# Hybrid scan and pooling block on one core: output weights kept in halves, transpositions queued behind a matmul, and two scan operations moved from GpSimd to VectorE

## The chip, the cores and the metric

The kernel runs on one core of one Trainium2 chip. The metric is the time on the device of one execution, in microseconds (us); the median of several executions is compared.

## What is computed

One layer of a hybrid block over 2048 tokens of 1024 channels (with 256 context tokens that only give the scan its initial state). In a short form, batch and context left out:

```python
h = modulate(rmsnorm(x, pre_norm_mix), shift, scale)
proj = h @ w_in                                   # z | x,B,C | dt | pooled channels
xs, bm, cm = split(silu(dwconv(proj[xBC], conv_w)))      # 5 taps, centred
y_f, _ = ssd_chunked(xs, dt_f, a_f, bm, cm, h0_f)         # chunks of 128, forward
y_b, _ = ssd_chunked(reversed ...)                         # the same, backward
y = rmsnorm((y_f + y_b + d_skip * xs) * silu(z), ssm_norm)
p = pool_mixer(proj[pool], w_pool, pool_scale)    # box means of 2, 4, 8, 16 on a 32 x 64 grid
yx = concat([y, p]) @ w_out                       # 1024 x 1024
x = x + gate1 * rmsnorm(yx, post_norm_mix)
h2 = modulate(rmsnorm(x, pre_norm_ffn), ...)
x = x + gate2 * rmsnorm((silu(g) * v) @ w_down)   # v, g = split(dwconv(h2 @ w_up)), 3 taps
```

In a chunked scan the state of a chunk is the state before it times a decay for each head, plus what the chunk adds; the output of a chunk is an inner part plus `C @ state`, scaled by a decay.

## The kernel before

**Products.** All large products are made of fp32 numbers split in a high and a low half in the type fp32r: `hi` is a copy in that type, `lo` the difference. `mm3` (line 152) makes a product of three matmuls: high by high, high by low, low by high. `split` (120) makes the halves: the copy on ScalarE where `he` is S, else on VectorE, the subtraction on the engine `le`. `wunit` (127) loads one unit of 128 x 1024 weights through SP into a buffer "w" (seven of them, `NW`), copies on ScalarE (line 122) and subtracts on GpSimd (line 125). With `kept` and `first` the halves are also stored in DRAM through SP (141); with `kept` and not `first` nothing is split, and the halves are loaded (143), each into its buffer "w". The input weights are used in this way (`win`, 148: block 0 stores, blocks 1 to 3 load). The output weights aren't kept: each of their 32 uses loads, copies and subtracts.

**Forward part.** The tokens are worked on in four blocks of 512, from 0 to 3. For each block the rows are normalised and transposed, multiplied with the input weights, convolved on VectorE (`conv`), and the four chunks of the scan follow (`chunks`, 499), spread between the matmuls of the next block. In `chunks`, `states` (464) makes what a chunk adds to the state and calls `step` (458), which multiplies the old state with its decay on GpSimd (460) and adds on VectorE (462). `y_off` (485) multiplies C with the state on TensorE, scales the result on VectorE (492) and adds it to y on GpSimd (493). y, the chunks' backward states, silu(z) and the pooled rows go to DRAM (`y_d`, `sb_d`, `sz_d`, `p_d`). Pooling (`pool_mix`, 589) is done beside the last block.

**Backward pass with the output projection.** Blocks 3 to 0. `back_load` (844) loads a block's y, states, C and silu(z) through SP. `back` (861) goes through its four chunks from the last to the first: `y_off` with the backward state, `step`, the multiplication with silu(z) on VectorE (873), squares on ScalarE (874); then a scaling of the rows (877). The rows are transposed (969), split into `hxh` and `hxl` (972), and multiplied with the output weights, two halves `hh` of 512 channels by four units of two `k` each. For block 3 the four pooled units come first, in a loop of their own (950 to 958), since pooling ends earlier than the scan. Behind each block `Post.finish` (824) makes x1 and stores it in `x1_d`; `norm_x1` (897) normalises x1 for the feed-forward and transposes it (910), spread between the next block's matmuls; for blocks 3 to 1 it writes `h_d`, which `quarter_sums` (887) and `load_operand` (931) read. `load_operand` brings a 128 x 512 piece into a buffer of "raw", "t512" (three) or "cacc" (three) by turns (`stage`, 923) and splits it into an operand `xc`. Operand T4 lies in the buffer "XB", which holds block 0's x1 rows before.

**Feed-forward.** `up_pair(1, i)` (1058) multiplies 22 pairs of weight units with the operands of blocks 2 and 3, in seven products each. The first takes the weights as they are, the second and others take sums of them, which VectorE makes into buffers "t512" and "cacc" (1067 to 1071). Block 0's rows are only normalised here: `norm_late(i)` (1038), four times, each in two steps placed behind a pair (1174 to 1182): the first loads x1 rows into a buffer "xr", squares them on ScalarE (1043) and scales them on VectorE (1045); the second transposes eight times on TensorE (1052), scales on ScalarE (1053) and stores.

**Order.** The order in which the source issues instructions isn't the order on an engine. A planner with a simulated time line orders each engine's instructions, by priority and by when it believes them ready; `hot()` (117) raises the priority by 500. On the chip each engine then runs its instructions in that order, and so does SP with its transfers.

Of the kernel before, what the change touches and what calls it, by code (L numbers as in the profile page):

```python
# [9 lines left out]
F32 = mybir.dt.float32  # L10
# [10 lines left out]
P = 128  # L21
# [4 lines left out]
TB = 512  # L26
NB = SEQ // TB
# [25 lines left out]
def hybrid_block(ctx: ExitStack, tc: tile.TileContext, x, cx, ccol, crow, par, rowpar, cst, edge,  # L53
                 w_ada_a, w_ada_b, w_in, w_dt, w_pool, w_out, w_up, w_down, out):
    nc = tc.nc
    V, S, G, PE = nc.vector, nc.scalar, nc.gpsimd, nc.tensor
# [14 lines left out]
    dp = ctx.enter_context(tc.tile_pool(name="dp", bufs=1, space=DRAM))  # L71
# [55 lines left out]
    def wunit(src, le=G, kept=None, first=True):  # L127
# [15 lines left out]
                        nc.sync.dma_start(out=t.bitcast(F32), in_=d_)  # L143
        return hi, lo

    wk_d = [[dp.tile([P, 1024], F32, name=f"wk_d{m}_{s}") for s in range(2)] for m in range(16)]

    def win(m, b):
# [3 lines left out]
    def mm3(o, lt, rt, start, stop, **kw):  # L152
        PE.matmul(o, lt[0], rt[0], start=start, stop=False, **kw)  # L153
        PE.matmul(o, lt[0], rt[1], start=False, stop=False, **kw)  # L154
        PE.matmul(o, lt[1], rt[0], start=False, stop=stop, **kw)  # L155

    def rstd(ss, n, d, p=P):

# [109 lines left out]
    ADD, MUL, SUB = ALU.add, ALU.mult, ALU.subtract  # L268
# [163 lines left out]
    def b64(ap):  # L432
        return ap.unsqueeze(2).to_broadcast([P, H, 64])
# [4 lines left out]
    def hv(ap):  # L438
        return ap.rearrange("p (h e) -> p h e", h=H)
# [17 lines left out]

    def step(new, old, dec, add):

        G.tensor_tensor(out=hv(new), in0=hv(old), in1=b64(dec), op=MUL)  # L460
        for dst, a in add:
            V.tensor_tensor(out=new[:, dst], in0=a, in1=new[:, dst], op=ADD)

# [21 lines left out]
    def y_off(ct, i, d, q, st, y):  # L485

        ps = pb()
        for g in range(2):
            PE.matmul(ps[:, g * 256:(g + 1) * 256], ct[:, g, :], st[:, g * 256:(g + 1) * 256],
                      start=True, stop=True)  # L490
        t = t512()[:, 0:DS]
        V.tensor_tensor(out=hv(t), in0=hv(ps), in1=b64(q["ecs"][:, d, i, :]), op=MUL)
        G.tensor_tensor(out=y, in0=y, in1=t, op=ADD)

    carry = {}

# [241 lines left out]
    for b in range(NB):  # L738
# [49 lines left out]
        for kk in range(KD // 2):  # L788
            u = win(12 + zord[2 * kk] // 2, b)
# [6 lines left out]
        for i in range(4):  # L796
            o = cacc()
# [121 lines left out]
    xc = {}  # L919
# [30 lines left out]
    for hh in range(2):  # L950
        po = quarters()
        for n_, k in enumerate((7, 6, 5, 4)):
            if n_ % 2 == 0:
                u = wunit(w_out[4 * hh + k // 2])
            for i in range(4):
                mm3(po[i], hx(k, 2 + i * P, 2 + (i + 1) * P), ut(u, k % 2, 512), n_ == 0, n_ == 3)
        for i in range(4):
            S.copy(out=ys[i][:, hh * 512:(hh + 1) * 512], in_=po[i])
    split_psum(NU2)

    for b in range(NB - 1, -1, -1):
# [26 lines left out]
        for hh in range(2):  # L988
            hs = slice(hh * 512, (hh + 1) * 512)
            kord = DN[4:] if b == NB - 1 else DN  # L990
            po = quarters()
            for n_ in range(0, len(kord), 2):
                u = wunit(w_out[4 * hh + kord[n_] // 2])
                for ip in (0, 2):
                    for k in kord[n_:n_ + 2]:
                        for i in (ip, ip + 1):
                            mm3(po[i], hx(k, 2 + i * P, 2 + (i + 1) * P), ut(u, k % 2, 512),
                                k == kord[0], k == kord[-1])
                if n_ or hh:
                    next(ngen, None)  # L1000
                    next(ngen, None)
                if b == 0 and n_ % 4 == 2:
                    load_operand(1, NAMES[2 * hh + n_ // 4])
            if b == NB - 1:
                for i in range(4):
                    with hot():
                        V.tensor_tensor(out=ys[i][:, hs], in0=po[i], in1=ys[i][:, hs], op=ADD)
                po = [ys[i][:, hs] for i in range(4)]
            pst.half(hh, po)
# [48 lines left out]
    def up_pair(p, i):  # L1058
# [16 lines left out]
        def product(o, a, n, start, stop):  # L1075

            with hot():
                w = wtile(F32R, "wo")
                if isinstance(a, int) and not p:
                    nc.sync.dma_start(out=w.bitcast(F32), in_=wu_d[i][a - 1])  # L1080
                else:
                    split(w[:, 0:512], w[:, 512:1024], sums[a - 1] if isinstance(a, int) else a, S, V)
            if isinstance(a, int) and p:
                G.dma_start(out=wu_d[i][a - 1], in_=w.bitcast(F32))
            for kk in range(4):
                ks = slice(kk * P, (kk + 1) * P)
                mm3(o, (w[:, 0:512][:, ks], w[:, 512:1024][:, ks]), (xc[n][:, kk, 0:TB], xc[n][:, 4 + kk, 0:TB]),
                    start and kk == 0, stop and kk == 3, skip_group_check=True)

        o = 1 - p  # L1090
# [18 lines left out]
        n = 2 * TB + o  # L1109
        acc = []  # L1110
        for j, u, a in zip((i, NFF + i), un, (wide("av", 2), stile([P, D + 4], "cr"))):
# [9 lines left out]
            for t in (1, 2):  # L1121
                V.scalar_tensor_tensor(out=a[:, 0:n], in0=u[:, t:t + n], scalar=pt[:, cw + t:cw + t + 1],  # L1122
                                       in1=a[:, 0:n], op0=MUL, op1=ADD)
# [47 lines left out]

    for n in NAMES[4:]:
        load_operand(1, n)
    side = []
    for i in range(4):
        side += [norm_late(i)] * 2
    for n_, i in enumerate(j + h * NK for j in range(NK) for h in range(2)):
        up_pair(1, i)
        if 1 <= n_ <= 8:
            next(side[n_ - 1])  # L1180
        if n_ in (12, 14, 16, 18):
            left_sums(n_ // 2 - 6)
    for n in NAMES:
# [193 lines left out]
```

## Time and profile before

| | before |
|---|---|
| median of 3 runs | 2281.81 us (2278.71 to 2284.29) |
| profiled execution, its own time | 2280.55 us |
| its span in the trace | 2278.8 us |
| mean granted clock of TensorE | 0.969 |
| busy: TensorE, VectorE, ScalarE, GpSimd | 2120.4, 1652.3, 899.0, 574.0 us |
| moved by transfers | 552.93 MB, 243 GB/s over the span |

A time in the trace counts from the span's start. The profile names TensorE's matmuls PE, its weight loads PEld, VectorE DVE, ScalarE ACT, GpSimd POOL and SyncE SP; L462 is line 462 of the kernel. "wl<-wst,wh" is an instruction that writes tile wl and reads wst and wh. An arrow "<-" behind an idle time names what ended it, as far as the semaphores tell. A clock of 1.00 is the higher of TensorE's two levels (2.4 GHz), 0.50 the lower (1.2 GHz), and a value between is a mean of the two over a stretch.

### The profile page before, as it was taken

Reading aid. Unit: us, or ns where it says so; the run is one execution under the profiler, and the core shown is the slowest. Engines: PE = TensorE matmul, PEld = TensorE weight load, DVE = VectorE, ACT = ScalarE, POOL = GpSimd, SP = SyncE. Lnnn points to the kernel's source line nnn. Section 1 sums busy time; section 2 is a strip of 40 time slices with the busy share of each in tenths; the row PEclk is TensorE's granted clock in tenths of the full one; section 3 lists DMA queues with packets and bytes.
Section 4 is the critical chain, followed back from the end, with each engine's and each line's share of the span. In section 5 each row is a group of like instructions: output and inputs, shape, how many; then the busy total and the mean of one; then the engine's idle time right before and its main releaser. Section 6 shows DMA issues by size and latency. Waiting matters only on the chain.

```text
span 2278.8 us, 27562 instructions
## 1 busy us (share of the span) xinstructions
PE 2120.4 (93%) x9473; PEld 1675.8 (74%) x9473; DVE 1652.3 (73%) x2500; ACT 899.0 (39%) x1405; POOL 574.0 (25%) x811
## 2 busy tenths in 40 slices
PE   8898999799679888599999998999999999999998
PEld 4695777687457666388888887888888888888876
DVE  5778779977678767688888977777777763333676
ACT  4334342333325545445444445333333333333433
POOL 1443624535355443111223210111111110000000
PEclk9899999899899999799999999999999999999999
DMA  7857969768765658755578657789898884444484
GB/s 298 276 205 255 302 216 365 254 224 280 254 231 171 223 196 316 245 218 197 213 250 292 233 201 261 264 296 330 300 331 294 301 289 142 146 141 139 146 272 141
DMA packets 250044, 552.93 MB, mean 243 GB/s; under 512 B 52976, under 2 KB 101808, under 8 KB 249392
## 3 DMA queue, kind: packets, MB, share of 16 engines
q1 hardware_dynamic: 212272, 425.86, 55.5%
q0 software_dynamic: 32320, 121.12, 13.6%
q10 hardware_dynamic: 5312, 4.20, 0.5%
q8 instruction: 74, 1.21, 0.2%
q14 instruction: 66, 0.54, 0.1%
HBM read 369.56 MB, written 181.54 MB: 242 GB/s over the span
## 4 chain that ended last, share of the span: by engine, by line
PE 55%; DMA 4%; DVE 3%; ACT 1%; issue 1%; POOL 0%; SPq 0%; ACTq 0%; DVEq 0%; POOLq 0%
PE pu L154 16%; PE pu L155 16%; PE pu L153 16%; PE pb L153 2%; PE pb L154 2%; PE pb L155 2%; DMA wst<-in_w_out_dram 1%; DMA h_d<-t 1%; DMA res<-x_d 0%; DMA XB<-h_d 0%; DVE accd L1258 0%; DVE accd L1240 0%; DMA stg<-ds_d 0%; DMA t<-ds_d 0%; DVE hxl L125 0%
## 5 line engine op out<-in xcount | busy, mean ns | idle before, releaser
L153 PE MATMUL pu<-xcT,wo 128*128 128x512 f32 x704 | 280.1, 398 | 0.4 <-ACT xcT L122 0.4
L154 PE MATMUL pu<-xcT,wo 128*128 128x512 f32 x704 | 279.4, 397 | 1.0 <-DVE xcT L125 1.0
L155 PE MATMUL pu<-xcT,wo 128*128 128x512 f32 x704 | 277.8, 396 | 0.0
L125 DVE TENSOR_TENSOR as<-ar,as 128x1024 fp32r<-128x1024 f32 x66 | 80.8, 1225 | 192.9 <-ACT as L122 192.8
L153 PE MATMUL pu<-xcB,wo 128*128 128x512 f32 x528 | 205.8, 397 | 4.7 <-ACT e L1096 4.7
L154 PE MATMUL pu<-xcB,wo 128*128 128x512 f32 x528 | 209.3, 396 | 0.0
L155 PE MATMUL pu<-xcB,wo 128*128 128x512 f32 x528 | 208.6, 397 | 0.0
L122 ACT CAST wo<-rawu 128x512 fp32r<-128x512 f32 x132 | 80.8, 621 | 238.3 <-PE pu L155 238.1
L153 PE MATMUL pu<-wh,hxh 128*128 128x512 f32 x384 | 152.4, 414 | 17.7 <-ACT wh L122 9.6
L154 PE MATMUL pu<-hxl,wh 128*128 128x512 f32 (+2 forms) x448 | 166.2, 372 | 2.9 <-DVE hxl L125 2.8
L155 PE MATMUL pu<-hxh,wl 128*128 128x512 f32 (+2 forms) x448 | 166.1, 373 | 2.0 <-POOL wl L125 2.0
L153 PE MATMUL pu<-hxh,wh 128*128 128x512 f32 (+2 forms) x448 | 165.2, 373 | 2.5 <-ACT wh L122 1.4
L125 POOL TENSOR_TENSOR wl<-wst,wh 128x1024 fp32r<-128x1024 f32 x48 | 118.9, 2477 | 186.5 <-ACT wh L122 173.5
L154 PE MATMUL pu<-wl,hxh 128*128 128x512 f32 x384 | 158.7, 413 | 6.8 <-POOL wl L125 6.8
L155 PE MATMUL pu<-wh,hxl 128*128 128x512 f32 x384 | 155.2, 412 | 2.7 <-DVE hxl L125 2.7
L153 PEld LDWEIGHTS pu<-xcT,wo 128*128 128x128 f32 x704 | 132.7, 188 | 33.4 <-ACT xcT L122 0.8
L154 PEld LDWEIGHTS pu<-xcT,wo 128*128 128x128 f32 x704 | 132.6, 188 | 33.4 <-DVE xcT L125 1.3
L155 PEld LDWEIGHTS pu<-xcT,wo 128*128 128x128 f32 x704 | 132.3, 188 | 32.4
L122 ACT CAST as<-ar 128x1024 fp32r<-128x1024 f32 x66 | 69.2, 1048 | 217.2 <-PE pb L155 211.4
L1122 DVE SCALAR_TENSOR_TENSOR av<-un,pt,av 128x1024 f32<-128x1024 f32 (+1 forms) x88 | 113.0, 1284 | 31.0 <-ACT av L1119 16.7
L330 DVE SCALAR_TENSOR_TENSOR cacc<-raw,pt,cacc 128x512 f32<-128x512 f32 (+1 forms) x152 | 132.4, 875 | 3.7
L154 PE MATMUL pu<-tc,as 128*128 128x512 f32 x330 | 130.6, 396 | 0.0
(374 smaller groups left out, 4947.7 us busy)
## 6 DMA issues: line engine op xcount, KB each, us to landing
wu_d<-wo POOLq DMA_DIRECT2D x88, 512.0 KB, 3.2
wo<-wu_d SPq DMA_DIRECT2D x88, 512.0 KB, 5.0
rawu<-in_w_up_dram SPq DMA_DIRECT2D x66, 512.0 KB, 4.9
wh<-wk_d SPq DMA_DIRECT2D x48, 512.0 KB, 7.2
wl<-wk_d SPq DMA_DIRECT2D x48, 512.0 KB, 5.9
ar<-s_d SPq DMA_DIRECT2D x44, 512.0 KB, 3.5
XB<-in_w_ada_b_dram SPq DMA_DIRECT2D x32, 512.0 KB, 6.1
wst<-in_w_out_dram SPq DMA_DIRECT2D x32, 512.0 KB, 4.7
```

Source lines behind the costliest of these rows:

```text
L122: S.copy(out=hi, in_=src)
L125: le.tensor_tensor(out=lo, in0=src, in1=hi.bitcast(F32), op=ALU.subtract)
L153: PE.matmul(o, lt[0], rt[0], start=start, stop=False, **kw)
L154: PE.matmul(o, lt[0], rt[1], start=False, stop=False, **kw)
L155: PE.matmul(o, lt[1], rt[0], start=False, stop=stop, **kw)
L330: V.scalar_tensor_tensor(out=a, in0=raw[:, j:j + t], scalar=pt[:, cw + j:cw + j + 1], in1=a, op0=MUL, op1=ADD)
L1122: V.scalar_tensor_tensor(out=a[:, 0:n], in0=u[:, t:t + n], scalar=pt[:, cw + t:cw + t + 1], in1=a[:, 0:n], op0=MUL, op1=ADD)
```

## The change

Three edits. (1) The output weights are kept like the input weights: their first use, in block 3, stores both halves in new DRAM tiles `wo_d`, and blocks 2 to 0 load them. (2) `mm3` returns its last matmul, and the products of `up_pair` keep the latest one in `mark`. The steps of `norm_late` are issued under `tc.issue_after`, so each TensorE instruction in them stands behind that matmul in TensorE's order; other engines' instructions get no such edge. (3) `step`'s multiplication and `y_off`'s addition are VectorE's in place of GpSimd's, in both directions of the scan and in the context.

```diff
+    wo_d = [[dp.tile([P, 1024], F32, name=f"wo_d{m}_{s}") for s in range(2)] for m in range(8)]
...
     def mm3(o, lt, rt, start, stop, **kw):
         PE.matmul(o, lt[0], rt[0], start=start, stop=False, **kw)
         PE.matmul(o, lt[0], rt[1], start=False, stop=False, **kw)
-        PE.matmul(o, lt[1], rt[0], start=False, stop=stop, **kw)
+        return PE.matmul(o, lt[1], rt[0], start=False, stop=stop, **kw)
...
     def step(new, old, dec, add):
-        G.tensor_tensor(out=hv(new), in0=hv(old), in1=b64(dec), op=MUL)
+        V.tensor_tensor(out=hv(new), in0=hv(old), in1=b64(dec), op=MUL)
...
         V.tensor_tensor(out=hv(t), in0=hv(ps), in1=b64(q["ecs"][:, d, i, :]), op=MUL)
-        G.tensor_tensor(out=y, in0=y, in1=t, op=ADD)
+        V.tensor_tensor(out=y, in0=y, in1=t, op=ADD)
...
             if n_ % 2 == 0:
-                u = wunit(w_out[4 * hh + k // 2])
+                u = wunit(w_out[4 * hh + k // 2], G, wo_d[4 * hh + k // 2])
...
             for n_ in range(0, len(kord), 2):
-                u = wunit(w_out[4 * hh + kord[n_] // 2])
+                m = 4 * hh + kord[n_] // 2
+                u = wunit(w_out[m], G, wo_d[m], b == NB - 1)
...
-                mm3(o, (w[:, 0:512][:, ks], w[:, 512:1024][:, ks]), (xc[n][:, kk, 0:TB], xc[n][:, 4 + kk, 0:TB]),
+                mark[0] = mm3(o, (w[:, 0:512][:, ks], w[:, 512:1024][:, ks]), (xc[n][:, kk, 0:TB], xc[n][:, 4 + kk, 0:TB]),
                     start and kk == 0, stop and kk == 3, skip_group_check=True)
...
-    side = []
+    mark, side = [None], []
...
         up_pair(1, i)
         if 1 <= n_ <= 8:
-            next(side[n_ - 1])
+            with tc.issue_after(mark[0].ins):
+                next(side[n_ - 1])
```

## Rows read from the trace of the kernel before

**Rows 1.** Busy time by stretch: length, then each engine's, TensorE's clock, transfers' share, GB/s.

```profile
200.00:580.00 380.00, 361.36 (x1686) 281.60 (x1685) 314.87 (x553) 132.97 (x209) 164.09 (x180) 0.98 0.80 268
...
360.00:400.00 40.00, 40.00 (x192) 31.60 (x190) 38.30 (x74) 12.54 (x23) 22.03 (x25) 1.00 1.03 364
...
577.00:707.00 130.00, 97.17 (x412) 71.24 (x411) 93.01 (x119) 45.20 (x76) 59.50 (x38) 0.89 0.64 217
...
707.00:932.00 225.00, 189.57 (x811) 147.22 (x810) 168.83 (x271) 110.93 (x207) 89.72 (x47) 0.93 0.69 240
...
860.00:932.00 72.00, 57.32 (x242) 43.87 (x241) 49.12 (x74) 36.07 (x68) 21.34 (x13) 0.93 0.86 311
```

**Rows 2.** TensorE's waits, 707 to 932 us: who waited for whom, total, times, longest.

```profile
PE pu L153 <- ACT wh L122: 9.6, 4, 5.2
PE pb L489 <- DVE hf L462: 7.2, 3, 3.7
PE pu L154 <- POOL wl L125: 6.8, 7, 1.7
PE pb L910 <- DVE XB L905: 3.5, 1, 3.5
PE pb L910 <- DVE eb L905: 3.2, 1, 3.2
```

**Rows 3.** The same view, 577 to 707 us.

```profile
PE pb L624 <- DVE XB L619: 15.7, 1, 15.7
PE pu L153 <- ACT XB L958: 4.0, 1, 4.0
```

**Rows 4.** Time line of GpSimd and of VectorE: start, length, instruction.

```profile
675.80 2.38 POOL L125 TENSOR_TENSOR wl<-wst,wh 128x1024 fp32r<-128x1024 f32 x1
...
675.87 2.86 DVE L873 TENSOR_TENSOR xt<-xt,BT 128x512 f32<-128x512 f32 x1 [1.16 <-POOL xt L493]
```

**Rows 5.** VectorE's groups, 707 to 932 us: count, busy us, mean ns, idle before.

```profile
L873 DVE TENSOR_TENSOR xt<-xt,BT 128x512 f32<-128x512 f32 x11 | 18.6, 1695 | 1.4 <-POOL xt L493 1.4
...
L462 DVE TENSOR_TENSOR hf<-ef,hf 128x512 f32<-128x512 f32 x9 | 9.2, 1026 | 0.6 <-POOL hf L460 0.6
```

**Rows 6.** The same view, 660 to 932 us: an instruction that reads PSUM.

```profile
L492 DVE TENSOR_TENSOR t<-pb,ecs 128x512 f32<-128x512 f32 x16 | 10.9, 680 | 0.1
```

**Rows 7.** GpSimd's groups, first three of 707 to 932 us, two of 200 to 580.

```profile
L125 POOL TENSOR_TENSOR wl<-wst,wh 128x1024 fp32r<-128x1024 f32 x24 | 59.6, 2483 | 99.7 <-ACT wh L122 86.8 <-PE pb L969 7.3 <-issue 5.1
L493 POOL TENSOR_TENSOR xt<-xt,t 128x512 f32<-128x512 f32 x10 | 16.3, 1636 | 7.5 <-DVE t L492 7.5
L460 POOL TENSOR_TENSOR hf<-hf,dec 128x512 f32<-128x512 f32 x8 | 11.1, 1390 | 3.7 <-DVE hf L462 3.7
...
L493 POOL TENSOR_TENSOR y<-y,t 128x512 f32<-128x512 f32 x12 | 17.4, 1452 | 8.5 <-DVE t L492 8.5
L460 POOL TENSOR_TENSOR hf<-hf,dec 128x512 f32<-128x512 f32 x12 | 16.4, 1363 | 20.5 <-PE pb L489 14.6 <-DVE hf L462 5.9
```

**Rows 8.** Transfers of the whole run: count, KB each, median us to landing.

```profile
wh<-wk_d SPq DMA_DIRECT2D x48, 512.0 KB, 7.2
...
wst<-in_w_out_dram SPq DMA_DIRECT2D x32, 512.0 KB, 4.7
```

**Rows 9.** SP's waits, 0 to 200 us, at the stores of the input weights.

```profile
SPq L141 <- ACT wh L122: 33.1, 9, 10.0
...
SPq L141 <- POOL wl L125: 14.0, 7, 3.2
```

**Rows 10.** Time lines of TensorE, ScalarE and VectorE at the feed-forward's start.

```profile
956.49 0.66 PE L1052 MATMUL pb<-cs_t,xr 128*128 128x128 f32 x2 [24.09 <-DVE xr L1045]
...
952.85 0.62 ACT L122 CAST xcT<-t 128x512 fp32r<-128x512 f32 x1 [0.30 <-DMA x_d<-XB]
...
954.98 0.69 DVE L125 TENSOR_TENSOR xcT<-t,xcT 128x512 fp32r<-128x512 f32 x1
...
956.86 0.69 DVE L1069 TENSOR_TENSOR t<-t,rawu 128x512 f32<-128x512 f32 x1
```

## The prediction

> **What bounds the kernel now.** I read the stretches first [rows 1], because the share of busy time over the whole run hides where TensorE stands. In the forward part from 200 to 580 us TensorE is busy 361.4 of 380 us. The feed-forward behind 962 us, more than half of the run, is untouched in its matmuls and I expect nothing from it. What is left is the backward pass with the output projection, 577 to 962 us. From 577 to 707 TensorE is busy 97.2 of 130 us (32.8 idle), and from 707 to 932 it is busy 189.6 of 225 (35.4 idle), at a granted clock of 0.93. Then follows one wait of 24.1 us [rows 10]. No engine is full there, so this is a stage of chains and queues, and the next view is who ended TensorE's waits.
>
> From 707 to 932 [rows 2] the list is: the high and low halves of the output weights, 9.6 + 6.8 = 16.4 us; the scan state (L462) 7.2; the normalised rows (L905) 3.5 + 3.2 = 6.7; the rest about 5. From 577 to 707 the largest is pooling, 15.7 us (L619), and then 4.0 us for ScalarE's copy at L958 [rows 3].
>
> The third view is the time line of GpSimd beside VectorE [rows 4]. GpSimd subtracts at 675.80 for 2.38 us; VectorE's multiplication L873 begins at 675.87 and takes 2.86 us. The same instruction size reading PSUM (L492) takes 0.680 us on average [rows 6], while L873 averages 1.695 and L462 1.026 us [rows 5]. So a VectorE instruction with two inputs in SBUF stands still while GpSimd works, and every GpSimd instruction in this pass costs VectorE's time too. VectorE's 168.8 us [rows 1] are partly such standing.
>
> **The change part by part.**
>
> *Kept output weights.* There are 32 uses of eight units. The first eight uses stay as they are and get two stores each; the other 24 lose one load, one ScalarE cast and one GpSimd subtraction, and get two loads. All 24 lie between 707 and 932 us: GpSimd's 24 subtractions there take 59.6 us [rows 7]. With the 10 additions (16.3) and 8 multiplications (11.1) that move, GpSimd loses 87.0 of its 89.7 us in that stretch [rows 1, 7], so nearly all the standing of VectorE goes. For L873 and L462 alone this returns 11 x (1.695 - 0.680) + 9 x (1.026 - 0.680) = 14.3 us. A unit's way shortens as well: now a load of 4.7 us, a cast and a subtraction of 2.48 us [rows 7, 8]; then a load, which for the input weights kept in the same way takes 7.2 us [rows 8]. About equal in length; the gain is that a unit holds two of the seven "w" buffers and not three, so the loads can be issued earlier, and that no unit queues on ScalarE or GpSimd. Of the 16.4 us I take 10 as gained and 6 as left, because the loads double.
>
> The price is transfers. From 707 to 932 us the queues move 240 GB/s at a share of 0.69 [rows 1], that is 54 MB, and 240 / 0.69 = 348 GB/s at a full share. 24 more pieces of 0.524 MB make 66.6 MB, or 191 us. The stretch can't become shorter than that: at most 34 us can be gained in it. Against the thought that full queues stop TensorE stands the stretch 360 to 400 us, with a share of 1.03, 364 GB/s and TensorE busy for all 40.0 us [rows 1].
>
> The stores stand on SP behind ScalarE and GpSimd. For the input weights SP stood 33.1 us in 9 waits for the high and 14.0 us in 7 for the low half [rows 9]. In the new place the loads of y, the pooled rows and the state stand behind them on SP. Bounds: nothing, if the planner issues them late enough, and 8 x (3.7 + 2.0) = 45 us if every pair waits as those did and TensorE waits for what is behind. I take 2 us, near the lower end, since pooling and not SP ends the large wait of this stretch [rows 3].
>
> *State decay and additions on VectorE.* From 707 to 932 us 18 instructions move. On VectorE one is as L462 undisturbed, about 0.69 us (0.680 for L492, [rows 6]): 18 x 0.69 = 12.4 us more against the 14.3 and more that are returned. VectorE's load does not grow. The chain from state to state loses a GpSimd step of 1.39 us [rows 7] and gets one of 0.69. So of the 7.2 us for the state and 6.7 us for the rows, both ended by VectorE, I take 10 as gained. From 577 to 707 us the same happens to 10 and 10 instructions; L958 there stands on ScalarE behind squares that wait for L873. I take 5 us of the 17.1 idle us besides pooling; less the 2 us for the stores, 3 us remain. Pooling's 15.7 us stay: its chain keeps its GpSimd steps.
>
> In the forward part 12 + 12 instructions move, 33.8 us of GpSimd [rows 7], for 24 x 0.69 = 16.6 us on VectorE, which is busy 314.9 of 380 us [rows 1]. Some standing is returned. Bounds: 6 us won (a third of the 18.6 idle us of TensorE) and 13 us lost, if TensorE's idle time grows by most of the addition. I take nothing: TensorE is the nearer bound there, and it covers VectorE as long as VectorE stays under it.
>
> *Clock.* At 0.93 over 225 us, 14% of the stretch, or 31.5 us, ran at the lower of the two levels (1.2 GHz in place of 2.4); matmuls in it took double the time, which costs at most 15.8 us. With two thirds of the waits gone I take 5.
>
> *Queued transpositions.* TensorE's order gets the transpositions of block 0's rows behind the third pair's matmuls, in place of ahead of the first pair's second product. The 24.1 us wait is written against them [rows 10]. But what they stood ahead of was not ready: the second product's weight sum L1069 starts at 956.86, later than the transposition at 956.49. That sum waits for a buffer "t512", which operand T4's pieces hold; these are cast only at 952.85, when the rows of x1 have landed and T4's own buffer is free, and subtracted from 954.98 [rows 10]. The edit orders TensorE only; ScalarE, VectorE and SP may keep their order. Bounds: 0 and 20 us (all but the time of the transpositions and of one cast). I take 1, near the end to which the row of L1069 points.
>
> **Sum.** 10 + 10 + 5 + 3 + 0 + 1 = 29 us off the profiled execution of 2280.55 us: 2251.5. The median of the runs, 2281.81, is 1.3 above it, so I forecast 2253 us.
>
> **The rivals.**
>
> *Transfers take over.* Between 860 and 932 us the share is 0.86 already [rows 1]: 61.9 us of full queues in 72, and 3.7 MB for seven more pieces at 348 GB/s make it 72.5. There the waits for weights stay and the clock with them: of the 29 us only the 10 by VectorE, the 3 and part of the weights remain, perhaps 14: 2268 us. For it: a third load is put on queues that are almost full. Against: the loads are issued earlier. The Trainium skill, "DMA: Bandwidth & Descriptors", section "Issuing engines are not separate DMA queues", says that transfers started by any engine share the same 16 DMA engines, so SP's and GpSimd's loads would not escape each other; the shares in the rows agree, since they are of all queues together.
>
> *The transpositions were the block.* If the planner, no longer offering them early, also brings the sums ahead of T4's pieces, the wait of 24.1 us shrinks to about 4: 20 us more, 2233 us.
>
> *Stalls only change place, or the queue edit does nothing and VectorE's additions eat the rest:* within 7 us of now, 2280 us. For it: every engine's order is made anew by the planner.
>
> *Slower: SP is stopped by the stores.* 45 us as above between 577 and 707, where p_d, y and state loads are behind the waiting stores; less the 26 us gained elsewhere: 2301 us. It decides from 26 / 8 = 3.2 us for each pair that TensorE really waits for. Against: the idle time there ends at VectorE, not at transfers [rows 3].
>
> **How the numbers follow.** Forecast 0.47, transfers 0.20, transpositions 0.15, no change 0.10, slower 0.08. Faster by over 0.3% (about 7 us, what a measurement can tell from no change here) is 0.47 + 0.20 + 0.15 = 0.82; within it 0.10; slower 0.08. The range goes down to 2213 (34 us at the floor of the transfers, 13 from 577 to 707, 20 at the transpositions and some of the 6 of the forward part) and up to 2280, which takes in the transfers' case and half of no change.
>
> **What would show it.** VectorE's L873 and L462 near 0.69 us in the last three blocks; GpSimd under 10 us from block 2 on; no TensorE wait for a cast or subtraction of output weights there, but perhaps for a landing; a share of transfers near 0.9 in the pass; the wait at the start of the feed-forward written against a weight sum or T4 in place of L1052, hardly shorter. I am wrong if the pass keeps its length with the shares of VectorE and transfers both under 0.8, if SP's waits for the stores stand ahead of TensorE's, or if the forward part grows by over 5 us.

## The result, and the profile after

| | before | after |
|---|---|---|
| median of 4 runs each, on one chip | 2281.44 us | 2259.15 us (2253.51 to 2261.42) |
| ratio, 95% interval | | 0.9898 [0.9876, 0.9921] |
| span of the profiled execution | 2278.8 us | 2258.7 us |
| mean granted clock | 0.969 | 0.968 |
| busy: TensorE, VectorE, ScalarE, GpSimd | 2120.4, 1652.3, 899.0, 574.0 us | 2113.3, 1625.1, 873.2, 424.2 us |
| moved | 552.93 MB | 573.91 MB |

The kernel became 22.3 us faster, where 28.8 were forecast. To see where, I cut both traces at the same four instructions: the start of block 3's last silu(z) store, TensorE's first transposition of block 3's rows (`xt`), the first product of the feed-forward, and that pair's second product (`xcT`). The lengths in us (the last row is each span):

| part | before | after | change |
|---|---|---|---|
| F: forward, to the last silu(z) store | 601.5 | 605.3 | +3.8 |
| G: pooled products, block 3's scan, to its transpositions | 87.7 | 90.3 | +2.6 |
| H: from there through blocks 2 to 0 to the first pair | 240.3 | 214.7 | -25.6 |
| I: first to second product of the first pair | 28.9 | 26.5 | -2.4 |
| J: the rest of the feed-forward | 1320.4 | 1321.9 | +1.5 |
| span | 2278.8 | 2258.7 | -20.1 |

So the last blocks gave 25.6 us, and the parts ahead of them took 6.4 back. The stretches of the kernel after, with the columns of [rows 1]; the pass now ends 20 us earlier, so its stretch ends at 912:

```profile
200.00:580.00 380.00, 357.57 (x1657) 279.90 (x1656) 319.45 (x569) 130.27 (x206) 125.89 (x156) 0.96 0.78 263
577.00:707.00 130.00, 98.71 (x408) 71.95 (x407) 94.58 (x140) 43.40 (x74) 30.50 (x18) 0.88 0.82 282
707.00:912.00 205.00, 182.14 (x836) 147.19 (x835) 135.82 (x306) 89.27 (x185) 5.72 (x6) 0.96 0.89 332
840.00:912.00 72.00, 55.69 (x243) 44.27 (x243) 40.16 (x90) 30.76 (x63) 3.05 (x5) 0.90 0.96 370
```

Read the third row against its answer in [rows 1]. TensorE idles 22.9 us in place of 35.4, at a clock of 0.96 in place of 0.93. VectorE is busy 33 us less although it executes 35 instructions more: this is standing that went. GpSimd does 5.7 us in place of 89.7. The price stands in the transfers: a share of 0.89 for 0.69, and 0.96 in the last 72 us.

TensorE's waits, from 707 to 912 us and then from 577 to 707, answer [rows 2, 3]:

```profile
PE pu L154 <- ACT wo L122: 9.2, 1, 9.2
PE pu L155 <- DMA wl<-wo_d: 6.5, 1, 6.5
PE pb L911 <- DVE eb L906: 5.1, 1, 5.1
```

```profile
PE pu L154 <- ACT hxh L122: 10.4, 2, 7.3
PE pb L625 <- DVE XB L620: 9.7, 1, 9.7
PE pb L970 <- issue: 4.8, 1, 4.8
```

No wait for a cast or a subtraction of output weights is left behind 707 us; of their 16.4 us one wait of 6.5 remains, for a landing. The state's 7.2 us are gone, of the rows' 6.7 one of 5.1 is left. The 9.2 us are the feed-forward's first weights, for which TensorE hadn't waited before. Ahead of 707 us a new wait stands at the top: block 3's pooled products wait 10.4 us for `hxh`.

VectorE's groups from 660 to 932 us, then L873 of the kernel before in the same stretch, then GpSimd's groups from 707 to 932 (as [rows 5 to 7]):

```profile
L463 DVE TENSOR_TENSOR hf<-ef,hf 128x512 f32<-128x512 f32 x16 | 15.0, 938 | 1.8 <-DMA ef<-sb_d 1.8
L874 DVE TENSOR_TENSOR xt<-xt,BT 128x512 f32<-128x512 f32 x16 | 12.4, 782 | 0.1
L494 DVE TENSOR_TENSOR xt<-xt,t 128x512 f32<-128x512 f32 x16 | 10.8, 684 | 2.5 <-DMA xt<-y_d 2.5
L461 DVE TENSOR_TENSOR hf<-hf,dec 128x512 f32<-128x512 f32 x15 | 10.2, 682 | 0.6 <-PE pb L490 0.5
```

```profile
L873 DVE TENSOR_TENSOR xt<-xt,BT 128x512 f32<-128x512 f32 x16 | 28.1, 1768 | 4.3 <-POOL xt L493 4.3
```

```profile
L125 POOL TENSOR_TENSOR wl<-wst,wh 128x1024 fp32r<-128x1024 f32 x1 | 2.4, 2391 | 6.9 <-ACT wh L122 6.9
```

L874 (L873 before) takes 782 ns on average for 1768, and both moved instructions 0.68 us, as the prediction had it. Of the 63 instructions in these four groups only three take more than 0.8 us: 2.27, 2.67 and 2.74, at 678.88, 691.15 and 712.59 us. Each of them begins while GpSimd is in one of its last subtractions of output weights, which start at 677.95, 690.92 and 712.39 us and take 2.3 to 2.7.

### The profile page after: what moved, and what is told of

Read it like the earlier page. It is cut to its first block, busy times and chain, and to the rows that moved or that the text cites. A ratio compares the mean times of both kernels' runs of the same rounds, so it can differ in the third digit from the quotient of the medians.

```text
span 2258.7 us, 27510 instructions
## 1 busy us (share of the span) xinstructions
PE 2113.3 (94%) x9473; PEld 1676.6 (74%) x9473; DVE 1625.1 (72%) x2566; ACT 873.2 (39%) x1379; POOL 424.2 (19%) x721
## 2 busy tenths in 40 slices
DMA packets 255804, 573.91 MB, mean 254 GB/s; under 512 B 53616, under 2 KB 102448, under 8 KB 255152
## 4 chain that ended last, share of the span: by engine, by line
PE 70%; DMA 7%; DVE 6%; issue 2%; ACT 2%; POOL 0%; SPq 0%; ACTq 0%; DVEq 0%; POOLq 0%
PE pu L154 20%; PE pu L155 20%; PE pu L156 20%; PE pb L154 2%; PE pb L155 2%; PE pb L156 2%; DVE cacc L331 1%; DVE junk L639 1%; PE pb L490 1%; DMA t<-h_d 1%; DMA wst<-in_w_out_dram 1%; PE pb L474 1%; DMA wl<-wo_d 1%; DMA cacc<-h_d 1%; DMA res<-x_d 1%
## 5 line engine op out<-in xcount | busy, mean ns | idle before, releaser
L154 PE MATMUL pu<-xcT,wo 128*128 128x512 f32 x704 | 280.2, 398 | 22.2 <-ACT wo L122 21.6
L154 PE MATMUL pu<-wh,hxh 128*128 128x512 f32 x384 | 151.3, 410 | 12.4 <-ACT hxh L122 10.4
L156 PE MATMUL pu<-wh,hxl 128*128 128x512 f32 x384 | 148.3, 400 | 0.0
L154 PE MATMUL pu<-tc,as 128*128 128x512 f32 x330 | 130.6, 396 | 0.0
L155 PE MATMUL pu<-tc,as 128*128 128x512 f32 x330 | 130.4, 395 | 0.0
L154 PEld LDWEIGHTS pu<-xcB,wo 128*128 128x128 f32 x528 | 100.4, 190 | 38.1 <-ACT wo L122 9.4
```

The lines of the kernel that those rows point to most:

```text
L156: return PE.matmul(o, lt[1], rt[0], start=False, stop=stop, **kw)
```

## The experiments

Lengths of the parts in all kernels, in us, with the median as a ratio to the kernel before that ran beside it:

| kernel | ratio, 95% interval | F | G | H | I | J |
|---|---|---|---|---|---|---|
| before | 1 | 601.5 | 87.7 | 240.3 | 28.9 | 1320.4 |
| after | 0.9898 [0.9876, 0.9921] | 605.3 | 90.3 | 214.7 | 26.5 | 1321.9 |
| e1_kept | 0.9911 [0.9888, 0.9935] | 606.7 | 83.9 | 223.3 | 26.0 | 1322.6 |
| e2_vector | 0.9977 [0.9965, 0.9990] | 609.3 | 83.1 | 235.4 | 28.4 | 1320.3 |
| e3_queued | 1.0008 [0.9994, 1.0023] | 600.5 | 88.3 | 241.1 | 29.1 | 1321.5 |
| e4_kept_vector | 0.9906 [0.9884, 0.9929] | 601.6 | 92.7 | 215.7 | 25.9 | 1321.9 |
| e5_gpsimd_busy | 1.0060 [1.0045, 1.0075] | 604.7 | 89.7 | 248.6 | 29.0 | 1322.8 |
| e6_more_transfers | 0.9966 [0.9955, 0.9976] | 604.3 | 92.9 | 227.1 | 29.6 | 1320.6 |
| e7_back_only | 0.9875 [0.9860, 0.9890] | 604.2 | 84.0 | 216.0 | 25.3 | 1321.3 |
| e8_own_sums | 0.9873 [0.9857, 0.9890] | 606.8 | 91.8 | 215.2 | 4.9 | 1335.0 |
| e9_gpsimd_busy2 | 1.0023 [1.0013, 1.0032] | 606.6 | 95.9 | 233.4 | 30.5 | 1322.6 |
| e10_back_and_sums | 0.9842 [0.9818, 0.9866] | 599.7 | 85.5 | 220.9 | 5.2 | 1332.1 |
| e11_stores_gpsimd | 0.9890 [0.9874, 0.9907] | 605.1 | 82.7 | 219.4 | 27.4 | 1319.5 |
| e12_one_half | 0.9875 [0.9860, 0.9890] | 604.4 | 90.8 | 211.8 | 24.7 | 1325.0 |

How far a part can be read: after, e4 and e8 have the same source up to the first pair; their F differ by 5.2 us, their G by 2.4 and their H by 1.0. So have e7 and e10: 4.5, 1.5 and 4.9. And e5, e6 and e12 have the source of the kernel after up to the end of G: over these six G runs from 89.7 to 92.9. A difference of up to 5 us in F or H of one pair of kernels says nothing, then, and one of 3 in G. Diffs are against the kernel after.

### One edit at a time

e1 keeps the output weights and nothing else; e2 has only the two operations on VectorE; e3 only the queued transpositions; e4 the first two without the third.

```diff
# e1: as e3 in step and y_off; e2: as e3 in both wunit calls; e1, e2 and e4:
-            with tc.issue_after(mark[0].ins):
+            if True:
# e3, in step and y_off, then in the two uses of w_out:
-        V.tensor_tensor(out=hv(new), in0=hv(old), in1=b64(dec), op=MUL)
+        G.tensor_tensor(out=hv(new), in0=hv(old), in1=b64(dec), op=MUL)
-        V.tensor_tensor(out=y, in0=y, in1=t, op=ADD)
+        G.tensor_tensor(out=y, in0=y, in1=t, op=ADD)
-                u = wunit(w_out[m], G, wo_d[m], b == NB - 1)
+                u = wunit(w_out[m])
```

> Kept output weights alone. Theory A (the gain comes from GpSimd work that VectorE stands still for, and from TensorE's waits for weight halves): GpSimd loses 24 subtractions, about 60 of 87 us of its work in blocks 2 to 0, and TensorE its 16 us of waits for halves; 12 to 20 us faster than before, about 2265. Theory B (the transfers take the gain): within 7 us of before, with waits for landings in place of waits for the casts.

> State decay and additions on VectorE alone. Theory A: the 34 us of multiplications and additions in blocks 2 to 0 no longer stop VectorE, but the 24 subtractions still do, and the forward part gets 17 us more VectorE work; 0 to 8 us faster than before, about 2277. Rival C (the short chain from state to state is what counts): 15 us or more faster. Rival D (VectorE's added work bounds the forward part): slower than before.

> Queued transpositions alone. Theory A: TensorE's wait of 24 us at the start of the feed-forward stays, now written against the weight sums or T4; 0 to 3 us faster than before, about 2280. Rival E (the transpositions were the block): the wait shrinks to under 8 us and the kernel is 15 to 20 us faster.

> The whole change without the queued transpositions. Theory A: 0 to 3 us slower than the whole change, about 2261. Rival E: 15 to 20 us slower, about 2276.

Measured: 2263.97, 2278.00, 2286.51 and 2262.55 us; the kernel before beside them 2283.76. The kept weights are worth 19.8 us, the two operations 5.8, the queue nothing that can be measured, with or without the others; the rivals B to E fell. In H the kept weights alone take off 17.0 us and the operations alone 4.9 (as much as two like kernels can differ); both together 24.6. There they add up. Over the whole run they don't: 25.6 us singly and 21.2 together (e4), and the difference lies in G.

VectorE's groups of e1 from 735 to 900 us show what the kept weights alone leave behind:

```profile
L463 DVE TENSOR_TENSOR hf<-ef,hf 128x512 f32<-128x512 f32 x7 | 8.5, 1215 | 0.7 <-POOL hf L461 0.7
L874 DVE TENSOR_TENSOR xt<-xt,BT 128x512 f32<-128x512 f32 x8 | 8.2, 1033 | 1.5 <-POOL xt L494 1.4
```

The scan's own GpSimd steps still stretch L463 and L874 to 1.2 and 1.0 us. And e2, from 707 to 932 us, shows why the operations alone are worth so little:

```profile
PE pu L155 <- POOL wl L125: 11.7, 8, 2.8
PE pu L154 <- ACT wh L122: 10.0, 5, 6.4
```

The state and most of the rows are gone from TensorE's waits, but the waits for weights grew from 16.4 to 21.7 us: a chain that becomes shorter runs into the next one. In e3 the wait at the feed-forward's start is written against the weight sum's cast. It is 26.2 us for 24.1, and I is as long as it was:

```profile
PE pu L154 <- ACT wo L122: 26.2, 1, 26.2
```

### GpSimd kept busy again

e5 adds, in blocks 2 to 0, a GpSimd addition of the two loaded halves of each unit; e9 adds hxh and hxl twice for each k, into a buffer that idles here. Nobody reads the results.

```diff
# e5, behind each unit's load
+                if b < NB - 1:
+                    G.tensor_tensor(out=scratch(BF16, D, "gj"), in0=u[0].bitcast(F32), in1=u[1].bitcast(F32), op=ADD)
# e9, for each k, twice
+                G.tensor_tensor(out=stile([P, 8, 80], "upad", 2).rearrange("p r c -> p (r c)")[:, 0:TB],
+                                in0=hxh[:, k, 2:2 + TB].bitcast(F32), in1=hxl[:, k, 2:2 + TB].bitcast(F32), op=ADD)
```

> The whole change, and in blocks 2 to 0 GpSimd adds the two loaded halves of each unit into a buffer that nobody reads: 24 instructions as long as the subtractions that went (about 2.4 us each, 58 us), and TensorE waits for none of them. Theory A1 (the gain comes mostly from VectorE no longer standing still for GpSimd): 8 to 15 us slower than the whole change, about 2270, with VectorE's instructions stretched again. Rival A2 (the gain comes from the weights' shorter way, and VectorE's standing is covered): less than 4 us slower, about 2261.

> The kernel after the change, with GpSimd kept busy again in blocks 2 to 0 without touching weight buffers: behind each of the eight k steps of each half it adds hxh and hxl into an idle buffer (upad) twice, 48 additions of 128x512 where nobody reads the result, about 50 to 60 us of GpSimd. Nothing else changes. This repeats the question of the run with additions on the loaded halves, which also held the buffers "w". Theory A1 (VectorE standing still beside GpSimd is the larger part of what the change returned): VectorE's two-input instructions are stretched again, the time comes 8 us or more above the kernel after, 2268 us or more. Theory A2 (the way of a weight unit and its buffers are the larger part): the stretching returns but costs under 4 us, about 2259 to 2263.

Measured: e5 2296.32 us, slower than the kernel before (2282.5). But this run mixes two causes: its additions read the weight buffers, so these came free later. SP waited 8.4 us for them, and TensorE 13.7 us for landings of the low half. By itself it can't tell the two causes apart. e9 puts the question without the weight buffers: of all waits from 690 to 940 us only two, of 0.8 and 0.2 us, end at an addition. e9: 2290.49 us, before 2285.56. Against the kernel after, scaled by its ratio (0.9898 x 2285.56 = 2262.2), that is 28 us more. The lines of e9: its additions (660 to 960 us), GpSimd and VectorE around 745 us, and the stretch 735 to 900; then the same stretch of the kernel after.

```profile
L965 POOL TENSOR_TENSOR upad<-hxh,hxl 128x512 f32<-128x512 f32 x48 | 68.8, 1459 | 107.6 <-DVE hxl L125 82.7 <-DVE r L167 23.3 <-DVE r L169 0.8
...
745.25 14.09 POOL L965 TENSOR_TENSOR upad<-hxh,hxl 128x512 f32<-128x512 f32 x8 [24.00 <-DVE hxl L125]
...
756.42 1.76 DVE L874 TENSOR_TENSOR xt<-xt,BT 128x512 f32<-128x512 f32 x1
...
761.56 0.68 DVE L874 TENSOR_TENSOR xt<-xt,BT 128x512 f32<-128x512 f32 x1
...
735.00:900.00 165.00, 136.50 (x616) 108.35 (x614) 124.83 (x222) 62.03 (x126) 60.88 (x44) 0.94 0.82 294
```

```profile
735.00:900.00 165.00, 151.33 (x699) 122.16 (x698) 102.29 (x224) 73.12 (x148) 3.33 (x5) 0.97 0.89 335
```

L874 takes 1.76 us while the additions run and 0.68 two us after they end. VectorE executes two instructions fewer than in the kernel after and is busy 22.5 us longer; TensorE does 14.8 us less in the same time. H grows by 18.7 us, as much as the kept weights alone had taken off it (17.0), with 68.8 us of GpSimd work against the 59.6 of [rows 7] that the kept weights removed. In blocks 2 to 0 no weight is loaded, cast or subtracted otherwise than in the kernel after. A1 stands: VectorE's standing beside GpSimd is enough to explain the larger part of the gain. That the shorter way of a unit gave nothing isn't shown by it. Two side effects remain in e9. G grew by 5.6 us too, since the first additions lie at 690 us already. And on GpSimd the additions stand ahead of one of block 3's subtractions and of the stores of the quarter sums; TensorE's waits end at neither, but its wait for landings is 10.5 us in place of 6.5. The Trainium skill, "SBUF — State Buffer", section "Who interferes with whom", says that a VectorE instruction with two SBUF inputs and a GpSimd one that reads SBUF exclude each other, and that the later one is stopped until the earlier is through; these rows agree, with 1.76 us against 0.68.

### More and fewer transfers

e6 lets GpSimd's queue store every loaded low half of blocks 2 to 0 once more (12.6 MB). e12 loads only the high half there and uses it in place of the low one as well, so the low half is left out of these products; 12.6 MB less.

```diff
# e6 ("dump" is a new DRAM tensor)
...
+                if b < NB - 1:
+                    G.dma_start(out=dump[m][b], in_=u[1].bitcast(F32))
# e12, in wunit with one = True for the uses that load
-            lo = main.tile([P, 1024], F32R, tag="w", name="wl", bufs=NW)
+            lo = hi if one else main.tile([P, 1024], F32R, tag="w", name="wl", bufs=NW)
-                for t, d_ in zip((hi, lo), kept):
+                for t, d_ in zip((hi,) if one else (hi, lo), kept):
```

> The whole change, and in blocks 2 to 0 the low half of each unit is stored once more by GpSimd's queue into a tensor that nobody reads: 24 more pieces of 0.52 MB, as many net as the change adds there, 12.6 MB. If the transfers' load is on the path (rival B): 12.6 MB at about 350 GB/s or 36 us of full queues, of which a good part is seen, 10 us or more slower. Theory A (covered as long as the share stays under 1): 0 to 5 us slower.

> The kernel after, with blocks 2 to 0 loading only the high half of the output weights and using it in place of the low half too, so the low half is left out of these products: 24 loads of 0.52 MB, 12.6 MB, and one buffer "w" a unit fewer, with the same matmuls. The mirror of the run with 12.6 MB more, which cost 16 us. If transfers bound the last blocks (theory B: the second load takes back part of the gain): 8 to 15 us below the kernel after, 2244 to 2251. If the load's price begins only where the queues are full (theory A): under 4 us, 2255 to 2259.

Measured: e6 2275.57 us, before 2282.5, some 16 us above the kernel after; e12 2256.99, before 2285.56, some 5 below. The stretch 735 to 900 us of e6, TensorE's waits there for landings (735 to 930) and one of SP's (690 to 930), then the stretch of e12:

```profile
735.00:900.00 165.00, 147.52 (x655) 117.90 (x654) 98.47 (x215) 65.11 (x132) 14.66 (x25) 0.93 0.97 379
...
PE pu L155 <- DMA wh<-wo_d: 5.6, 1, 5.6
PE pu L156 <- DMA wl<-wo_d: 4.4, 4, 2.2
...
SPq L143 <- DMA dump<-wl: 4.7, 2, 2.6
```

```profile
735.00:900.00 165.00, 152.11 (x713) 123.28 (x711) 108.19 (x240) 78.01 (x158) 3.33 (x5) 0.98 0.76 269
```

With 12.6 MB more the share is 0.97 and H grows by 12.4 us; with as much less the share falls to 0.76 and H shrinks by 2.9, no more than two like kernels differ. Theory A, which priced more transfers at 0 to 5 us, falls with e6; theory B's 8 to 15 us for fewer fall with e12, whose 5 lie just outside theory A's 4. The two steps are unequal, as if a bend lay above the share of 0.89. But the runs are no exact mirror: e6 adds stores and holds each low half until its store has read it (the 4.7 us of SP's waits), and e12 frees a weight buffer for each unit. So the bend is not shown, and the 5 us of e12, an upper bound for the second load's price, hold both causes. The clock has a part in e6: it is 0.93 in this stretch, where the kernel after has 0.97.

### Where the forward part and G lost

e7 leaves the two operations on GpSimd in the forward scans. e11 issues the 16 stores of the output weights from GpSimd's queue.

```diff
# e7 (the context's step likewise)
-            step(hn, hf, q["dec"][:, 0, i, :], parts)
+            step(hn, hf, q["dec"][:, 0, i, :], parts, G)
...
-        V.tensor_tensor(out=y, in0=y, in1=t, op=ADD)
+        (V if d else G).tensor_tensor(out=y, in0=y, in1=t, op=ADD)
# e11, in wunit with q_ = G for w_out
-                        nc.sync.dma_start(out=d_, in_=t.bitcast(F32))
+                        q_.dma_start(out=d_, in_=t.bitcast(F32))
```

> The whole change, but the forward scans' decay and additions stay on GpSimd; only the backward pass has them on VectorE. Theory A (the forward part lost 4 to 8 us by them): the forward part ends at about 601 us as before, and the kernel is 2 to 6 us faster than the whole change, about 2255. Rival: the loss up to there is the planner's order, not VectorE's load; within 2 us.

> The kernel after, with the 16 stores of the output weights' halves in block 3 issued by GpSimd's queue and not by SP. If SP, standing for the halves at these stores, delays the loads behind them and this is what the stretch 577 to 735 us lost (rival): 5 to 10 us below the kernel after. If it is not (the prediction took 2 us for it): 3 us or less in either direction, 2256 to 2262 us.

Measured: e7 2253.71 us, before 2282.5, some 5 us below the kernel after by the ratios, though their intervals meet. e11 2259.24, before 2285.56, some 2 below: within the 3 us of its second expectation and not the rival's 5 to 10. In e7 F ends only 1.1 us earlier than in the kernel after, and G is 6.3 us shorter: the gain that I had looked for in the forward part lies in G. In e11, too, G is shorter, by 7.6 us, while H is longer by 4.7, which two like kernels can differ by. SP's time line in the kernel after, from 672 us, and what two kinds of its waits ended at (577 to 735 us):

```profile
672.18 0.33 SPq L883 DMA_DIRECT2D cacc<-p_d  x1
677.12 0.33 SPq L141 DMA_DIRECT2D wo_d<-wh  x1
679.64 0.54 SPq L851 DMA_DIRECT2D CT<-ct_d  x1
681.17 0.37 SPq L859 DMA_DIRECT2D BT<-sz_d  x1
...
685.99 0.36 SPq L859 DMA_DIRECT2D BT<-sz_d  x1
...
SPq L141 <- ACT wh L122: 18.2, 6, 5.7
...
SPq L859 <- DVE xt L874: 5.9, 4, 3.3
```

After 672.5 us SP stands at the store of a high half until ScalarE has cast it. But the loads behind this store are not block 3's. They bring C of block 1 (the third of four such loads) and silu(z) and the states of block 2, into buffers that block 3 still uses, and each starts as soon as an instruction of block 3 frees its buffer. The two of silu(z) start at 681.17 and 685.99 us, where two of block 3's L874 end at 681.15 and 685.96; the states at 683.58, where L463 ends at 683.55. So these loads wait for block 3's chain and not the chain for them, and that SP's standing at the stores costs the time isn't shown; in e7 SP stands there for casts 14.4 us, and G is short. What the traces show is another order on VectorE, first in the kernel after, then in e11:

```profile
668.76 0.69 DVE L125 TENSOR_TENSOR hxl<-cacc,hxh 128x512 fp32r<-128x512 f32 x1 [6.51 <-ACT hxh L122]
669.40 0.69 DVE L463 TENSOR_TENSOR hf<-ef,hf 128x512 f32<-128x512 f32 x1
...
682.87 0.68 DVE L463 TENSOR_TENSOR hf<-ef,hf 128x512 f32<-128x512 f32 x1
...
691.15 2.67 DVE L463 TENSOR_TENSOR hf<-ef,hf 128x512 f32<-128x512 f32 x1 [1.75 <-DMA ef<-sb_d]
...
694.99 1.68 DVE L878 TENSOR_SCALAR xt<-xt,r 128x512 f32<-128x512 f32 x4
```

```profile
662.57 0.69 DVE L463 TENSOR_TENSOR hf<-ef,hf 128x512 f32<-128x512 f32 x1 [3.17 <-DMA ef<-sb_d]
...
671.42 0.69 DVE L463 TENSOR_TENSOR hf<-ef,hf 128x512 f32<-128x512 f32 x1
...
684.60 1.67 DVE L878 TENSOR_SCALAR xt<-xt,r 128x512 f32<-128x512 f32 x4
```

In the kernel after, block 3's first state step (669.40) stands behind the subtraction of a pooled row's low half, which waits 6.5 us for its cast; in e11 it comes ahead of it (662.57). Block 3's fourth and last step then comes 11 us later (682.87 against 671.42). Between it and the scaling of block 3's rows (L878), which the transpositions need, VectorE has block 2's first step (691.15): it waits for its states and then takes 2.67 us, with GpSimd's subtraction of 690.92 beside it. The transpositions come at 695.6 us, in e11 at 687.8.

This goes through all kernels. With the stores on SP and the forward scans' operations on VectorE (after, e4, e5, e6, e8, e12, and e9 with its additions) block 3's first step stands behind that subtraction, and G is 89.7 to 92.9 us, in e9 95.9. With one of the two edits undone (e1, e2, e7, e10, e11) it stands ahead, and G is 82.7 to 85.5. With neither (before, e3) it stands ahead, and G is 87.7 and 88.3. So each edit alone shortens G by some 4 us, and the pair lengthens it by 3. The planner makes this order; why it does so for the pair alone, and whether the order is the whole of the difference, was not separated: no run forces one order under the same edits.

As for F: the last silu(z) store of block 1 starts between 327.5 and 333.2 us in the five kernels with the forward operations on GpSimd and between 336.4 and 340.1 in the nine with them on VectorE. The means are 330.0 and 338.6, and those of F 602.5 and 605.3. So block 1 loses 9 us, and blocks 2 and 3 give two thirds of it back or more: the 3 us that remain are less than like kernels differ by (599.7 to 606.7 us in the five, 601.6 to 609.3 in the nine).

### The sums at the feed-forward's start

e8 gives the first pair's four weight sums the buffers "av" and "cr", which are free; e10 has this and e7's edit.

```diff
-                s1, s2, s3, s4 = sums = [t512()[:, 0:512], t512()[:, 0:512], cacc(), cacc()]
+                if i == 0:
+                    b1, b2 = wide("av", 2), stile([P, D + 4], "cr")
+                    sums = [t[:, c0:c0 + 512] for t in (b1, b2) for c0 in (0, 512)]
+                else:
+                    sums = [t512()[:, 0:512], t512()[:, 0:512], cacc(), cacc()]
+                s1, s2, s3, s4 = sums
```

> The whole change, but the first pair's four weight sums lie in buffers of their own that are idle at that time (one av, one cr) and not in t512 and cacc, which the operands' pieces hold. Theory A (the wait of 21.7 us at the start of the feed-forward is for a buffer): the sums are made when their weights land, about 910 us, the wait shrinks to under 12 us, and the kernel is 8 to 14 us faster than the whole change, about 2248. Rival G (the operands themselves, T2 and T1, are as late as the sums): within 3 us.

> The kernel after, with two of the earlier edits together: in the forward scans the two operations stay on GpSimd (only the backward pass has them on VectorE), and the first pair's four weight sums have buffers that are free (av, cr) in place of t512 and cacc. Alone they gave 5.5 and 5.3 us. If the two gains lie in different stretches and add up (theory A: each stretch is its own chain, the forward part's loss being carried to the end): about 10 to 11 us below the kernel after, 2248 to 2249 us. If they share slack further on: under 7 us, 2252 us or more.

TensorE, VectorE and ScalarE in the kernel after, then TensorE's waits of e8 from 905 to 950 us:

```profile
936.82 0.80 PE L154 MATMUL pu<-xcT,wo 128*128 128x512 f32 x1 [21.65 <-ACT wo L122]
...
933.19 0.68 DVE L125 TENSOR_TENSOR xcT<-t,xcT 128x512 fp32r<-128x512 f32 x1
...
933.86 0.68 DVE L1070 TENSOR_TENSOR t<-rawu 128x512 f32<-128x512 f32 x1
...
936.15 1.13 ACT L122 CAST wo<-t 128x512 fp32r<-128x512 f32 x2
```

```profile
PE pu L154 <- ACT wo L122: 8.9, 1, 8.9
PE pu L154 <- ACT e L1103: 5.0, 1, 5.0
PE pu L154 <- ACT xcT L122: 3.1, 1, 3.1
```

Measured: e8 2253.88 us, before 2282.5, some 6 us below the kernel after by the ratios, where 8 to 14 were expected. In the kernel after the first sum starts as soon as the last operand piece has left its buffer "t512" (933.86); with buffers of its own the sums' wait of 21.65 us is gone and I shrinks by 21.6 us. But J grows by 13.1: the operands themselves come later (the last piece is subtracted at 950.0 us in place of 936.3), and part of the wait moves to the following products, as the 3.1 and the 5.0 us show; the 8.9 stand ahead of the first product, as in the kernel after. e10: 2249.17 us, before 2285.56, 0.9842 [0.9818, 0.9866]; against the kernel after 0.9842 / 0.9898 = 0.9943, about 13 us. By the times the two edits add up, as theory A had it, and e10 is the fastest kernel of this study.

## Why the prediction was right, and where its steps were not

The forecast was 2253 us within 2213 to 2280; measured were 2259.15. It was right that the last blocks carry the gain, and in the main why. That the sum of their terms met H to within a microsecond is in part luck. The columns of [rows 1], cut at the marks of H, before and then after:

```profile
689.20:929.45 240.25, 204.00 (x881) 159.06 (x880) 181.87 (x275) 117.52 (x217) 104.28 (x55) 0.94 0.68 236
```

```profile
695.58:910.30 214.72, 191.51 (x880) 155.12 (x880) 142.85 (x313) 94.07 (x194) 8.43 (x7) 0.95 0.89 330
```

- *Kept weights and VectorE's chains, 10 + 10 us.* Of the 16.4 us of waits for weights 9.9 went, of the 13.9 for state and rows 8.8. But the wait of 9.2 us for the feed-forward's first weights came in their place, which no term had. TensorE's idle time in H fell from 36.3 to 23.2 us: 13.0 us where the two terms had 20. The other 12.5 of the 25.6 us lie in TensorE's own instructions, as many as before in less time. Between the two edits e1 and e2 put 17.0 and 4.9 us in H, so my split was uneven: the removed subtractions also freed VectorE, and e9 shows that this freeing is enough for the larger part.
- *Clock, 5 us.* At 0.93 and then 0.96, 31.5 of 225 us ran at the lower level before and, worked out in the same way, 0.08 x 205 = 16.4 after. Half of each is the most that was lost, 15.8 and 8.2, which would give 7.6 back. Counted in H, 41 of 672 matmuls of 128x512 began at the lower level before, and 9 after. In the kernel after such matmuls start every 0.43 us at the lower level (around 913 us) and every 0.23 at the higher (around 914.5), so 32 fewer give 6.4 us, as an estimate. The term held. Some 6 of the 12.5 us are left that no term had and no run assigns.
- *577 to 707 us, 3 us gained.* This step failed: G grew by 2.6, and by some 3 over like kernels. The 5 us for the moved operations held: e11, which has them and no store on SP, has a G 5.0 us shorter than the kernel before. The term that was mis-sized is the 2 us for the stores, which stand for some 7 between the kernels with both edits and those with one undone (by whole kernels 2 us in e11 and 5 in e7). Its working had the path wrong, too, and so had the rival of the stopped SP with its 45 us: both counted loads that stand behind the stores, but the loads found there wait for block 3's own chain, and what grew is that chain, in another order on VectorE. The remark that came nearest is that the planner makes every engine's order anew. That the price appears only with the forward operations on VectorE was in no step.
- *Forward part, nothing.* It lost 3.8 us in the profiled execution; over all kernels the means differ by 2.8, less than like kernels do. But TensorE doesn't cover VectorE there all the way, as I had said: where block 1's scan runs, the additions come through, 9 us, and most of it is made up later. It lay inside the bounds of -6 and 13.
- *Queued transpositions, 1 us.* e3 and e4 show none. The row of the sum, which waits for a buffer "t512", pointed to the right block; e8 confirms it, and shows that only some 8 of the 21.65 us can be had in this way, since the operands are next.
- *Transfers.* The floor wasn't reached, and the rival that transfers take over (2268 us) didn't come true. But the thought behind its small chance, that full queues needn't stop TensorE, has a limit: e6 lost 12.4 us in H at a share of 0.97, if in part by the buffers that its stores hold.

By spans, 29 us were summed up and 20.1 measured. The 8.9 missing are 5.6 in G (-2.6 for 3), 3.8 in F and 1.5 in J, less 0.6 in H and 1.4 in I, which gave more than their terms.

## What to carry to other kernels

Work on GpSimd that no one waits for cost here what VectorE stood beside it: before counting an operation as off the path, compare the same instruction's mean with one that reads PSUM, and count the difference as part of that operation's price. Before a late load is called a cause, look at what freed its buffer: behind the stores in block 3 the loads that came late were waiting for the very chain that they seemed to hold up. Where a planner makes the orders, two edits that each gain can lose as a pair: compare the order on the engine that ends the wait. And when two chains end the waits by turns, an edit that shortens one alone returns a part of its waits: read the sum of both lists, and test the pair.

## What the runs showed that was not expected

More transfers cost more than fewer gave back. Around the same kernel (share 0.89, 335 GB/s from 735 to 900 us), 12.6 MB less gave 2.9 us in H (0.76, 269 GB/s), and 12.6 MB more cost 12.4 (0.97, 379 GB/s). A bend would explain it, but with buffers held and freed beside it that isn't shown.

Small instructions stand as well. In e9 two steps of the rows' norm (L168), of 128 x 4 elements, take 0.24 us together, and 1.35 us when a GpSimd addition has begun beside them:

```profile
772.43 0.24 DVE L168 SCALAR_TENSOR_TENSOR r<-r,r 128x4 f32<-128x4 f32 x2
...
773.61 1.35 DVE L168 SCALAR_TENSOR_TENSOR r<-r,r 128x4 f32<-128x4 f32 x2
...
773.65 2.55 POOL L965 TENSOR_TENSOR upad<-hxh,hxl 128x512 f32<-128x512 f32 x2 [14.30 <-DVE r L167]
```

So two small steps lost 1.1 us here, nearly as much as L874 beside the additions (1.76 for 0.68).
